# adaLN weights of a diffusion block in wider tiles, with different columns in TensorE's column groups

## The chip, the cores and the metric

One core of a Trainium2 chip runs the whole program. The metric is its device time in microseconds, from the first instruction to the last; lower is better. TensorE does the matrix products, VectorE, ScalarE and GpSimd the work on elements, and SyncE issues the transfers of the weights.

## What is computed

One block of a diffusion backbone, for 256 latent tokens and 256 context tokens of 2048 channels, in float32. The condition c gives six vectors of 2048 by one matrix product (adaLN), a shift, a scale and a gate for the attention and for the MLP:

```
m = silu(c) @ w_ada + b_ada              # w_ada 2048 x 12288; also for c_ctx
shift_a, scale_a, gate_a, shift_m, scale_m, gate_m = split(m, 6)
h = rms_norm(x) * (1 + scale_a) + shift_a        # context: with c_ctx
q, k, v, u = split(h @ w_in)                     # 2048 x 2560
x = x + gate_a * (concat(attention(q, k, v), pooling(u)) @ w_out)
h = rms_norm(x) * (1 + scale_m) + shift_m
x = x + gate_m * (relu(h @ w_up) ** 2 @ w_down)  # hidden 8192
out = rms_norm(x)                                # latent tokens
```

The product with w_ada has only two rows, c and c_ctx, but its matrix is 100 MB, a third of all that is read.

## The kernel before

**Weights** come as one ordered stream of tiles [128, 4, 512] float32, 1 MB each: four row blocks (of 128 rows of the matrix) by 512 columns. Up to five tiles (N_RAW) are in the buffer, and SyncE issues a tile's transfers (L76) when one comes free. A tile of a main product is split in halves ahead of its use: ScalarE makes the high part hi (L89), VectorE or, for every third half of the first 140 tiles, GpSimd the low part lo (L91). A main product is three matmuls, hi by hi, lo by hi, hi by lo (mm3, L280 to L282). An adaLN tile isn't split.

**An adaLN chunk before** is 256 columns of a scale beside the same 256 of a shift, which serves two row blocks of the activations, or 512 columns of a gate. Its four tiles have four row blocks each. On TensorE (ada_pe, L297) a tile is four matmuls of 32 columns of silu(c) by 512 of the weights, one on each column group (tile_position (0, 32 j)), each for another row block; so the four groups hold partial sums of the same 512 columns. After the fourth tile ScalarE copies the bank (ada_e, L303), and four small matmuls by the constant sel (ada_cols, L327, the "column step" below) add up the partial sums and put the columns on the partitions; ada_scale and ada_shift (L332 to L336) finish. For a gate one matmul by the constant selb (L502) adds up and spreads over all partitions instead. On VectorE (ada_dve, L317 and L319) a tile is four operations of 512 columns that add weights times a scalar into ada_v.

**Order of the stages.** The input projection goes through w_in in five groups of row blocks (2, 2, 4, 4, 4), accumulating with VectorE (L428). Among the products of a group stand the adaLN tiles whose scale and shift the next group needs; after a chunk's last one, `modulated` (L445 to L448) scales, shifts and splits two row blocks. Before the last group all 32 attention tiles have been used. The 48 late tiles follow a table, ADA_LATE: MLP chunks 0 and 1 and the gate's four on TensorE, MLP 2, 3, 4, 6 and 7 on VectorE, 5 on TensorE. Of them 4 tiles go beside the last q products, 20 into the attention, 12 into the output projection, 4 behind the first tile of the up projection and 8 further on in it.

The output projection (ps_w) ends in a gate product and an addition for each half of the tokens (t, L816; x, L818), squares (L819), transpositions (L797), the norm's factor spread by a matmul (diag L830, ps_r L832) and copied (rb, L834). `modulate_m` (L846 to L849) makes the MLP's operands mhi and mlo of four row blocks. The first three groups of the up projection run at once, by row blocks, 48 products for each of the twelve tiles, so that the last shifts and scales can come late. The late adaLN tiles of that stage may start only behind rb.

On each engine the order is that of a scheduler, which simulates the program and puts instructions where it expects them to be ready. Each engine then works strictly in that order. TensorE may stand before an instruction that waits, while later ones would be ready.

Of the kernel before, what the change touches and what calls it, by code (L numbers as in the profile page):

```python
# [8 lines left out]
F32 = mybir.dt.float32  # L9
# [42 lines left out]
class WeightStream:  # L52
    """One ordered stream of float32 weight tiles of four blocks [128, 512].

    Tiles are loaded in order, N_RAW deep. Those of the main products are split
    ahead of their use, two blocks at a time, into two float32r parts
    (hi + lo == w exactly).
    """
# [36 lines left out]
    def next(self, kind):  # L95
        """The next tile: the raw one, or W(j, cols) -> the parts of block j."""
# [20 lines left out]
def kernel(  # L117
# [17 lines left out]
    # ------------------------------------------------------------ weight stream  # L135
# [15 lines left out]
    # the input projection's schedule, with the first shift and scale in pairs of row blocks  # L151
    def group_ops(g, pairs):
# [5 lines left out]
        ada = [op for c in pairs for op in [("ada", c, kg) for kg in range(4)] + [("mod", c)]]  # L158
# [8 lines left out]
    in_ops = group_ops(0, [1]) + group_ops(1, [2, 3]) + group_ops(2, [4, 5]) + group_ops(3, [6, 7])  # L167
    last = group_ops(4, [])
    late = [(what, j, kg) for what, j, _ in ADA_LATE for kg in range(4)]

    def add_ada_pair(c_, kg, scale, shift):
# [862 lines left out]
```

## Time and profile before

| | |
|---|---|
| median of 3 runs (1180.76 to 1180.92) | 1180.92 us |
| span of the profiled execution | 1180.8 us |
| TensorE busy | 1128.4 us (96%) |
| VectorE busy | 806.4 us (68%) |
| ScalarE busy | 509.2 us (43%) |
| GpSimd busy | 145.8 us (12%) |
| read and written by transfers | 286.75 MB, mean 243 GB/s |
| chain of work that ended last | TensorE 74%, VectorE 13%, transfers 7% |

In the table the share of busy time is a mean over stages with different limits, so each stage has to be read by itself. The records of matmuls overlap, since they are pipelined; what one costs is the time until the next one's start. A float32 matmul shows as two records. In the rows PE is TensorE, DVE VectorE, ACT ScalarE, POOL GpSimd and PEld the loading of weights into TensorE.

### The profile page before, as it was taken

To read this page: it belongs to the slowest core of one execution; us is meant where nothing else is said; L and a number is where in the kernel's file an instruction comes from. 1 tells how busy PE (TensorE), PEld (TensorE's weight loads), DVE (VectorE), ACT (ScalarE), POOL (GpSimd) and SP (SyncE) were. 2 spreads that over 40 slices of the span, in tenths; PEclk is the share of its full clock that TensorE was granted. 3 is DMA by queue.
4 is the path that set the end of the run, shared out by engine and by line. 5 is a ranking of instruction groups with operands and counts; after the bars stand their busy time and mean duration, and the time that the engine had idled before them with its cause. 6 is when DMAs were issued, how large, how long until landed. Compare 5 with 4: busy or idle time off the path is not lost.

```text
span 1180.8 us, 17728 instructions
## 1 busy us (share of the span) xinstructions
PE 1128.4 (96%) x7140; PEld 952.2 (81%) x7140; DVE 806.4 (68%) x1203; ACT 509.2 (43%) x760; POOL 145.8 (12%) x98
## 2 busy tenths in 40 slices
PE   3999999989999979999999999999999999999996
PEld 2767788746588769988989989989989989988984
DVE  4645468988698888897765765774554554576576
ACT  4633233277633433365434434533533533543452
POOL 1111123610143312320000000000000000000001
PEclk9899999999999979899999999999999999999998
DMA  9999898577898899968675775775566555565532
GB/s 338 312 336 342 279 326 276 178 268 263 272 350 278 288 328 322 319 229 284 243 278 179 249 263 184 254 262 178 179 191 193 187 178 181 185 195 189 179 107 72
DMA packets 174017, 286.75 MB, mean 243 GB/s; under 512 B 5608, under 2 KB 72352, under 8 KB 172784
## 3 DMA queue, kind: packets, MB, share of 16 engines
q1 hardware_dynamic: 172800, 279.55, 70.7%
q0 software_dynamic: 848, 5.55, 1.3%
q8 instruction: 56, 0.92, 0.3%
q10 hardware_dynamic: 288, 0.52, 0.1%
q14 instruction: 25, 0.20, 0.0%
HBM read 283.50 MB, written 2.10 MB: 242 GB/s over the span
## 4 chain that ended last, share of the span: by engine, by line
PE 74%; DVE 13%; DMA 7%; issue 3%; ACT 1%; SPq 1%; POOL 1%; DVEq 0%; ACTq 0%
PE ps_d L282 10%; PE ps_d L281 10%; PE ps_d L280 10%; PE ps_up L282 9%; PE ps_up L280 9%; PE ps_up L281 9%; PE ps_ada L297 4%; DVE ada_v L319 4%; DVE lo L91 4%; DMA raw<-in_w_in_dram 2%; PE ps_qu L280 2%; DMA raw<-in_w_mlp_up_dram 2%; DMA raw<-in_w_out_dram 2%; PE ps_qu L282 2%; PE ps_qu L281 2%
## 5 line engine op out<-in xcount | busy, mean ns | idle before, releaser
L91 DVE TENSOR_TENSOR lo<-raw,hi 128x1024 fp32r<-128x1024 f32 x293 | 376.7, 1300 | 233.5 <-ACT hi L89 233.3
L89 ACT CAST hi<-raw 128x1024 fp32r<-128x1024 f32 x330 | 337.7, 1049 | 416.6 <-PE ps_d L282 159.4
L280 PE MATMUL ps_up<-mhi,hi 128*128 128x256 f32 x1024 | 292.0, 287 | 0.6 <-ACT hi L89 0.6
L282 PE MATMUL ps_up<-mhi,lo 128*128 128x256 f32 x1024 | 289.5, 285 | 1.4 <-DVE lo L91 1.4
L281 PE MATMUL ps_up<-mlo,hi 128*128 128x256 f32 x1024 | 290.1, 284 | 0.0
L281 PE MATMUL ps_d<-lo,ahi 128*128 128x512 f32 x512 | 200.5, 394 | 0.0
L280 PE MATMUL ps_d<-hi,ahi 128*128 128x512 f32 x512 | 200.5, 394 | 0.0
L280 PEld LDWEIGHTS ps_up<-mhi,hi 128*128 128x128 f32 x1024 | 197.4, 193 | 2.7 <-issue 1.8
L282 PE MATMUL ps_d<-hi,alo 128*128 128x512 f32 x512 | 199.5, 395 | 0.0
L282 PEld LDWEIGHTS ps_up<-mhi,lo 128*128 128x128 f32 x1024 | 196.8, 193 | 2.2 <-DVE lo L91 2.1
L281 PEld LDWEIGHTS ps_up<-mlo,hi 128*128 128x128 f32 x1024 | 197.5, 193 | 1.1 <-issue 1.0
L319 DVE SCALAR_TENSOR_TENSOR ada_v<-raw,c_sil,ada_v 128x512 f32<-128x512 f32 x135 | 124.7, 923 | 22.0 <-DMA raw<-in_w_ada_dram 20.1
L91 POOL TENSOR_TENSOR lo<-raw,hi 128x1024 fp32r<-128x1024 f32 x37 | 95.4, 2580 | 336.4 <-ACT hi L89 316.9
L282 PEld LDWEIGHTS ps_d<-hi,alo 128*128 128x128 f32 x512 | 96.5, 188 | 22.4
L280 PEld LDWEIGHTS ps_d<-hi,ahi 128*128 128x128 f32 x512 | 96.5, 188 | 22.2
L281 PEld LDWEIGHTS ps_d<-lo,ahi 128*128 128x128 f32 x512 | 96.5, 188 | 22.1
L280 PE MATMUL ps_qu<-hhi,hi 128*128 128x256 f32 x256 | 75.6, 296 | 5.9 <-ACT hhi L447 5.9
L297 PE MATMUL ps_ada<-raw,c_sil 128*32 128x512 f32 x480 | 74.3, 629 | 2.0 <-DMA raw<-in_w_ada_dram 1.9
L281 PE MATMUL ps_qu<-hlo,hi 128*128 128x256 f32 x256 | 72.7, 285 | 0.0
L282 PE MATMUL ps_qu<-hhi,lo 128*128 128x256 f32 x256 | 72.1, 285 | 0.0
L950 POOL DMA_DIRECT2D fw<-in_final_norm_w_dram x1 | 0.6, 571 | 576.3 <-DVE lo L91 576.3
L280 PEld LDWEIGHTS ps_qu<-hhi,hi 128*128 128x128 f32 x256 | 49.4, 193 | 24.4 <-issue 11.5
(189 smaller groups left out, 1275.2 us busy)
## 6 DMA issues: line engine op xcount, KB each, us to landing
raw<-in_w_ada_dram SPq DMA_DIRECT2D x128, 512.0 KB, 7.7
raw<-in_w_mlp_up_dram SPq DMA_DIRECT2D x64, 1024.0 KB, 5.5
raw<-in_w_mlp_down_dram SPq DMA_DIRECT2D x64, 1024.0 KB, 5.1
raw<-in_w_ada_dram SPq DMA_DIRECT2D x32, 1024.0 KB, 6.6
raw<-in_w_in_dram SPq DMA_DIRECT2D x19, 1024.0 KB, 6.7
raw<-in_w_out_dram SPq DMA_DIRECT2D x16, 1024.0 KB, 7.0
xnat<-in_x_dram SPq DMA_DIRECT2D x2, 1024.0 KB, 6.1
xnat<-in_ctx_dram SPq DMA_DIRECT2D x2, 1024.0 KB, 12.2
```

Of the source, the lines that this page charges most:

```text
L89: nc.scalar.copy(hi, raw)
L91: eng.tensor_tensor(lo, raw, hi.bitcast(F32), ALU.subtract)
L280: nc.tensor.matmul(ps, a[0], b[0], start=first, stop=False, skip_group_check=True)
L281: nc.tensor.matmul(ps, a[0], b[1], start=False, stop=False, skip_group_check=True)
L282: nc.tensor.matmul(ps, a[1], b[0], start=False, stop=last, skip_group_check=True)
L297: nc.tensor.matmul(ps[32 * j : 32 * j + 32, :], c_sil[:, 4 * kg + j, :], raw[:, j, :], start=(kg == 0), stop=(kg == 3), tile_position=(0, ...
L319: nc.vector.scalar_tensor_tensor(box["e"], raw[:, j, :], sc, box["e"], ALU.mult, ALU.add)
L950: nc.gpsimd.dma_start(out=fw, in_=final_w.partition_broadcast(P))
```

## The change

The tiles keep their 1 MB, their number (80) and the places where they stand between the steps. What changes is which part of w_ada a tile holds, and what is done with it.

- **Attention's scale and shift.** Five chunks (ADA_CHUNKS) in place of eight, with the row blocks of the five groups of the input projection: 2, 2, 4, 4, 4. The chunks of two are as before. One of four is 512 columns of the scale beside 512 of the shift, in eight tiles of two row blocks, with rows of 2 KB, not 1 KB. The column groups then hold different columns and, for the two row blocks, two partial sums. `modulated` runs for all four row blocks behind a chunk.
- **Gate.** Sixteen tiles of one row block by all 2048 columns (8 KB rows). Each column group holds 512 other columns and the whole sum. At the end four matmuls of 32 rows, on the four row groups, spread it.
- **MLP's scale and shift.** The first eight row blocks are one chunk "M" of sixteen tiles (1024 columns of each, one row block a tile) on TensorE; the column step is four matmuls for all eight. Blocks 8 to 11 and 12 to 15 are chunks "m" of eight tiles on VectorE, with two operations of 1024 columns a tile in place of four of 512, and a column step of eight matmuls.
- The late table now begins with the gate. So the last 8 tiles of "M" and the first 4 of the chunk for blocks 8 to 11 fall into the output projection, the other 4 of it behind the first up tile. TensorE has 32 of the 48 late tiles (28 before), VectorE 16 (20).
- The buffer t of the gate product has two copies, not three; am and sm keep only the column for c.

```diff
-ADA_LATE = (
-    ("m", 0, "pe"), ("m", 1, "pe"),
-    ("g", 0, "pe"), ("g", 1, "pe"), ("g", 2, "pe"), ("g", 3, "pe"),
-    ("m", 2, "dve"), ("m", 3, "dve"), ("m", 4, "dve"), ("m", 5, "pe"), ("m", 6, "dve"), ("m", 7, "dve"),
-)
+ADA_CHUNKS = ((0, 2), (2, 2), (4, 4), (8, 4), (12, 4))
+ADA_LATE = (("g", 0, 16), ("M", 0, 16), ("m", 8, 8), ("m", 12, 8))
...
-    in_ops = group_ops(0, [1]) + group_ops(1, [2, 3]) + group_ops(2, [4, 5]) + group_ops(3, [6, 7])
+    in_ops = group_ops(0, [1]) + group_ops(1, [2]) + group_ops(2, [3]) + group_ops(3, [4])
...
-    def add_ada_pair(c_, kg, scale, shift):
-        ks = slice(4 * kg, 4 * kg + 4)
-        S.add("ada", *((lambda t, o=o: t[:, :, o : o + 256], w_ada_v[:, ks, col + 256 * c_ : col + 256 * c_ + 256])
-                       for o, col in ((0, scale), (256, shift))))
+    def add_ada_pair(k0, n, i, scale, shift):
+        w, nk = P * n, 8 // n
+        S.add("ada", *((lambda t, o=o: t.rearrange("p a b -> p (a b)").rearrange("p (k c) -> p k c", k=nk)[:, :, o : o + w],
+                        w_ada_v[:, nk * i : nk * i + nk, col + P * k0 : col + P * k0 + w])
+                       for o, col in ((0, scale), (w, shift))))
...
+                S.add("ada", (lambda t: t.rearrange("p a b -> p (a b)"), w_ada_v[:, i, G_A : G_A + D]))
...
             for j in range(4):
                 nc.tensor.matmul(
-                    ps[32 * j : 32 * j + 32, :], c_sil[:, 4 * kg + j, :], raw[:, j, :],
-                    start=(kg == 0), stop=(kg == 3), tile_position=(0, 32 * j),
+                    ps[32 * j : 32 * j + 32, :], c_sil[:, nk * i + j // n, :], raw[:, j, :],
+                    start=(i == 0), stop=(i == steps - 1), tile_position=(0, 32 * j),
...
+    def ada_dve_m(finish):
+            raw = S.next("ada").rearrange("p (k n) c -> p k (n c)", k=2)
+            for j in range(2):
+                sc = c_sil[:, 2 * i + j, 0:1]
...
+                    nc.vector.scalar_tensor_tensor(box["e"], raw[:, j, :], sc, box["e"], ALU.mult, ALU.add)
...
-        for j in range(4):
-            nc.tensor.matmul(ps[:, 2 * j : 2 * j + 2], e[:, 128 * j : 128 * j + 128], weights, start=True, stop=True)
+        n, w = e.shape[1] // P, weights.shape[1]
+        for j in range(n):
+            nc.tensor.matmul(ps[:, w * j : w * j + w], e[:, P * j : P * j + P], weights, start=True, stop=True)
...
-                    nc.tensor.matmul(ps, spread, e, start=True, stop=True)
+        def finish_g(e):
+            for j in range(4):
+                ps = bank("ps_g")
+                r = slice(32 * j, 32 * j + 32)
+                nc.tensor.matmul(ps, selb[r, :], e[r, :], start=True, stop=True, tile_position=(32 * j, 0))
...
+            k0, n = ADA_CHUNKS[op[1]]
+            for p_ in range(k0 // 2, (k0 + n) // 2):
+                modulated(p_)
...
-            t = wop.tile([P, 512], F32, tag="t", name="t", bufs=3)
+            t = wop.tile([P, 512], F32, tag="t", name="t", bufs=2)
```

The order that the scheduler builds, on TensorE where the third group of w_in begins (blocks 4 to 7; ps_k and ps_v are its k and v products). Before:

```order
L280 MATMUL ps_k<-hhi,hi 128x512
L281 MATMUL ps_k<-hlo,hi 128x512
L297 MATMUL ps_ada<-raw,c_sil 32x512 x4
L280 MATMUL ps_k<-hhi,hi 128x512
L281 MATMUL ps_k<-hlo,hi 128x512
L280 MATMUL ps_v<-hi,hhi 128x256 x2
L282 MATMUL ps_k<-hhi,lo 128x512
```

and after:

```order
L281 MATMUL ps_k<-hhi,hi 128x512
L300 MATMUL ps_ada<-raw,c_sil 32x512
L281 MATMUL ps_k<-hhi,hi 128x512
L281 MATMUL ps_v<-hi,hhi 128x256 x2
L300 MATMUL ps_ada<-raw,c_sil 32x512 x3
L282 MATMUL ps_v<-lo,hhi 128x256 x2
L300 MATMUL ps_ada<-raw,c_sil 32x512 x4
L282 MATMUL ps_k<-hlo,hi 128x512
```

The products on the high parts (hhi) now go ahead, two adaLN tiles stand among them, one of them as 1 and 3 matmuls, and the first product on a low part (hlo) comes behind both.

On TensorE in the norm, from the last transpositions to the first up products, before:

```order
L797 MATMUL tp_x<-ident,x_3274 128x128 x8
L832 MATMUL ps_r<-diag,ones 128x256
L327 MATMUL ps_adac<-ones,ada_v 128x2 x4
L297 MATMUL ps_ada<-raw,c_sil 32x512 x16
L280 MATMUL ps_up<-mhi_4045,hi 128x256 x2
L281 MATMUL ps_up<-mlo_4046,hi 128x256
```

and after, with the end of the first up tile:

```order
L836 MATMUL tp_x<-ident,x_3217 128x128 x8
L871 MATMUL ps_r<-diag,ones 128x256
L281 MATMUL ps_up<-mhi_3972,hi 128x256 x2
L282 MATMUL ps_up<-mlo_3973,hi 128x256
...
L283 MATMUL ps_up<-mhi_3987,lo 128x256
L347 MATMUL ps_adac<-ones,ada_v 128x1 x8
L281 MATMUL ps_up<-mhi_3972,hi 128x256
```

The column step and the four tiles ahead of the first up product are gone; the eight matmuls of the column step for blocks 8 to 11 stand behind its 48 products.

On VectorE from the copy of the norm's factor on, before:

```order
L834 COPY rb<-ps_r 128x256
L846 SCALAR_TENSOR_TENSOR x2T_3282<-x2T_3282,am,rb 128x256 x4
L846 SCALAR_TENSOR_TENSOR x2T_3283<-x2T_3283,am,rb 128x256 x4
L332 TENSOR_TENSOR am<-ps_adac,bcol 128x4
L336 TENSOR_TENSOR sm<-ps_adac,bcol 128x4
L849 SCALAR_TENSOR_TENSOR mlo_4046<-x2T_3282,sm,mhi_4045 128x256
L317 TENSOR_SCALAR ada_v<-raw,c_sil 128x512
```

and after:

```order
L873 COPY rb<-ps_r 128x256
L322 SCALAR_TENSOR_TENSOR ada_v<-raw,c_sil,ada_v 128x1024
L885 SCALAR_TENSOR_TENSOR x2T_3225<-x2T_3225,am,rb 128x256 x4
L885 SCALAR_TENSOR_TENSOR x2T_3226<-x2T_3226,am,rb 128x256 x4
L322 SCALAR_TENSOR_TENSOR ada_v<-raw,c_sil,ada_v 128x1024
L888 SCALAR_TENSOR_TENSOR mlo_3973<-x2T_3225,sm,mhi_3972 128x256
...
L322 SCALAR_TENSOR_TENSOR ada_v<-raw,c_sil,ada_v 128x1024 x3
L89 TENSOR_TENSOR lo<-raw,hi 128x1024
L322 SCALAR_TENSOR_TENSOR ada_v<-raw,c_sil,ada_v 128x1024 x3
```

Eight sums of 1024 columns for the column step stand here now, among the operations that make the MLP's operands (x2T, mlo) and one low part of a weight tile.

## Rows read from the trace of the kernel before

**Rows 1.** Windows: start:end and length us; busy PE, PEld, DVE, ACT, POOL (xcount); PEclk, DMA share, GB/s.

```profile
32.00:211.00 179.00, 179.00 (x1304) 137.98 (x1304) 108.18 (x188) 67.25 (x94) 41.28 (x26) 0.99 0.94 312
211.00:250.00 39.00, 31.29 (x213) 23.57 (x212) 38.43 (x83) 17.12 (x44) 19.47 (x23) 0.96 0.55 188
250.00:317.00 67.00, 64.78 (x422) 35.89 (x421) 54.14 (x149) 47.84 (x117) 4.76 (x2) 1.00 0.74 258
317.00:412.50 95.50, 95.41 (x442) 77.66 (x441) 80.86 (x80) 37.91 (x50) 37.34 (x17) 1.00 0.90 310
412.50:430.00 17.50, 10.63 (x50) 5.17 (x50) 14.41 (x44) 5.82 (x14) 0.57 (x1) 0.61 0.94 307
430.00:509.30 79.30, 76.28 (x605) 74.97 (x602) 67.78 (x83) 32.29 (x43) 23.97 (x9) 0.96 0.90 305
```

**Rows 2.** Waits of TensorE, 32 to 211 us: total us, times, longest.

```profile
PE ps_qu L280 <- ACT hhi L447: 5.9, 1, 5.9
```

**Rows 3.** Timeline of TensorE: start us, duration us, instructions; adaLN pieces and a product.

```profile
62.48 1.05 PE L297 MATMUL ps_ada<-raw,c_sil 128*32 128x512 f32 x2
...
76.74 1.06 PE L297 MATMUL ps_ada<-raw,c_sil 128*32 128x512 f32 x8
77.74 0.39 PE L280 MATMUL ps_qu<-hhi,hi 128*128 128x256 f32 x1
```

**Rows 4.** Timeline of TensorE: a column step, a gate matmul, and what follows each.

```profile
177.03 0.95 PE L327 MATMUL ps_adac<-sel,ada_e 128*128 128x2 f32 x8
177.84 0.36 PE L280 MATMUL ps_qu<-hhi,hi 128*128 128x256 f32 x1
...
262.00 1.02 PE L502 MATMUL ps_g<-ada_e,selb 128*128 128x512 f32 x2
262.95 0.64 PE L297 MATMUL ps_ada<-raw,c_sil 128*32 128x512 f32 x4
```

**Rows 5.** Timeline of VectorE: the modulation of two row blocks.

```profile
178.41 1.38 DVE L445 TENSOR_SCALAR xT<-xT,am_a,sm_a 128x256 f32<-128x256 f32 x4
```

**Rows 6.** Timeline of TensorE, 416 to 437 us.

```profile
416.10 2.35 PE L797 MATMUL tp_x<-ident,x 128*128 128x128 f32 x8 [3.69 <-DVE x L818]
...
424.22 6.01 PE L297 MATMUL ps_ada<-raw,c_sil 128*32 128x512 f32 x32
430.16 0.50 PE L280 MATMUL ps_up<-mhi,hi 128*128 128x256 f32 x2
...
436.02 0.95 PE L327 MATMUL ps_adac<-sel,ada_e 128*128 128x2 f32 x8
```

**Rows 7.** Timeline of VectorE, 411 to 431 us.

```profile
411.17 1.22 DVE L91 TENSOR_TENSOR lo<-raw,hi 128x1024 fp32r<-128x1024 f32 x1
412.31 2.32 DVE L319 SCALAR_TENSOR_TENSOR ada_v<-raw,c_sil,ada_v 128x512 f32<-128x512 f32 x3
414.54 0.68 DVE L816 TENSOR_TENSOR t<-ps_w,ga 128x512 f32<-128x512 f32 x1
...
422.83 0.42 DVE L834 COPY rb<-ps_r 128x256 f32<-128x256 f32 x1 [1.31 <-PE ps_r L832]
423.29 3.26 DVE L846 SCALAR_TENSOR_TENSOR x2T<-x2T,am,rb 128x256 f32<-128x256 f32 x8
...
426.60 0.47 DVE L849 SCALAR_TENSOR_TENSOR mlo<-x2T,sm,mhi 128x256 fp32r<-128x256 f32 x1
...
430.24 0.74 DVE L319 SCALAR_TENSOR_TENSOR ada_v<-raw,c_sil,ada_v 128x512 f32<-128x512 f32 x1
```

**Rows 8.** Waits of TensorE, 430 to 509.3 us: total us, times, longest.

```profile
PE ps_up L282 <- DVE lo L91: 1.4, 2, 0.8
PE ps_adac L327 <- DVE ada_v L319: 1.0, 1, 1.0
```

**Rows 9.** Windows, columns as in rows 1: two stretches with different adaLN row lengths.

```profile
60.00:90.00 30.00, 30.00 (x220) 20.29 (x219) 15.06 (x26) 9.57 (x12) 5.16 (x2) 1.00 0.99 336
260.00:265.00 5.00, 5.00 (x29) 2.56 (x28) 3.98 (x9) 4.87 (x9) 0.15 (x1) 1.00 1.05 385
```

More of the change, by code (lines that the diff above doesn't have):

```diff
@@ L157, in group_ops @@
             prod = prod[4:8] + [("ctx",)] + prod[8:] + prod[:4]
-        ada = [op for c in pairs for op in [("ada", c, kg) for kg in range(4)] + [("mod", c)]]
+        ada = [op for c in pairs for op in [("ada", c, i) for i in range(2 * ADA_CHUNKS[c][1])] + [("mod", c)]]
         ops, done = [], 0
@@ L189, in add_in @@
         elif op[0] == "late":
[L190 removed]
+            what, j, i = late.pop(0)
             if what == "g":
[L192 removed]
+                S.add("ada", (lambda t: t.rearrange("p a b -> p (a b)"), w_ada_v[:, i, G_A : G_A + D]))
             else:
[L194 removed]
+                add_ada_pair(j, 8 if what == "M" else 4, i, SC_M, SH_M)
         elif op[0] == "pool":
@@ L254 @@
     sel = const.tile([P, 2], F32, name="sel")
+    sel2 = const.tile([P, 2, 2], F32, name="sel2")
     cols = const.tile([P, P], F32, name="cols")
@@ L282, in mm3, with ada_pe, step @@
         nc.tensor.matmul(ps, a[1], b[0], start=False, stop=last, skip_group_check=True)
-    def ada_pe(finish):
+    def ada_pe(nk, finish):
         box = {}
-        def step(kg):
-            if kg == 0:
+        steps, n = KC // nk, 4 // nk
+        def step(i):
+            if i == 0:
                 box["ps"] = bank("ps_ada")
@@ L371 @@
     nc.vector.tensor_tensor(sel, sel, ident[:, 96:98], ALU.add)
+    for j in range(2):
+        nc.vector.tensor_tensor(sel2[:, j, :], ident[:, 32 * j : 32 * j + 2], ident[:, 64 + 32 * j : 66 + 32 * j], ALU.add)
     nc.vector.tensor_copy(selb, sel[:, 0:1].broadcast_to([P, P]))
@@ L484, in project_qu @@
         accumulate(dst, ps, g == 0)
-    am = const.tile([P, KC, 2], F32, name="am")
-    sm = const.tile([P, KC, 2], F32, name="sm")
+    am = const.tile([P, KC, 1], F32, name="am")
+    sm = const.tile([P, KC, 1], F32, name="sm")
     gate = {}
     def late_steps():
-        for what, j, engine in ADA_LATE:
-            ada, weights, spread = (ada_pe, sel, selb) if engine == "pe" else (ada_dve, ones[:, 0:2], ones)
-            def finish(e, what=what, j=j, weights=weights, spread=spread):
-                if what == "m":
-                    k = slice(2 * j, 2 * j + 2)
-                    ps = ada_cols(e, weights)
-                    ada_scale(am[:, k], ps[:, 0:2], bcol[:, 64 + 2 * j : 66 + 2 * j], cols[:, 48 + 2 * j : 50 + 2 * j])
-                    ada_shift(sm[:, k], ps[:, 2:4], bcol[:, 48 + 2 * j : 50 + 2 * j])
-                else:
-                    ps = bank("ps_g")
-                    nc.tensor.matmul(ps, spread, e, start=True, stop=True)
-                    gs = gate["a"][:, 512 * j : 512 * j + 512]
-                    nc.vector.tensor_tensor(gs, ps, gs, ALU.add)
-            steps = ada(finish)
-            yield from steps[:4]
-            late_finish.append(steps[4])
@@ new lines, in scale_shift @@
+        def scale_shift(k0, scale, shift):
+            n = scale.shape[1]
+            k = slice(k0, k0 + n)
+            ada_scale(am[:, k], scale, bcol[:, 64 + k0 : 64 + k0 + n], cols[:, 48 + k0 : 48 + k0 + n])
+            ada_shift(sm[:, k], shift, bcol[:, 48 + k0 : 48 + k0 + n])
+        def finish_g(e):
[3 more added lines that the diff above has]
+                nc.tensor.matmul(ps, selb[r, :], e[r, :], start=True, stop=True, tile_position=(32 * j, 0))
+                gs = gate["a"][:, 512 * j : 512 * j + 512]
+                nc.vector.tensor_tensor(gs, ps, gs, ALU.add)
@@ new lines, in late_steps, with finish_M, finish_m @@
+        for what, k0, n in ADA_LATE:
+            def finish_M(e, k0=k0):
+                ps = ada_cols(e, ident[:, ::32])
+                for h in range(2):
+                    scale_shift(k0 + 4 * h, ps[:, :, h : h + 1], ps[:, :, 2 + h : 3 + h])
+            def finish_m(e, k0=k0):
+                ps = ada_cols(e, ones[:, 0:1])
+                scale_shift(k0, ps[:, 0:4], ps[:, 4:8])
+            steps = ada_pe(1, finish_g) if what == "g" else ada_pe(1, finish_M) if what == "M" else ada_dve_m(finish_m)
+            yield from steps[:n]
+            late_finish.append(steps[n])
```

41 lines of the change are left out of this document (25 added, 16 removed).

## The prediction

> **What bounds the kernel now.** I read the busy time by stage first, where each row's busy time of TensorE is to be set against the stage's length [rows 1]. TensorE is busy 179.00 of 179.00 us in the input projection, 95.41 of 95.50 in the output projection, 64.78 of 67.00 while the attention goes over into it and 76.28 of 79.30 in the first up projection. There, a matmul more or less is time more or less. Two stretches are otherwise. From 211 to 250 us VectorE has 38.43 of 39.00 us and TensorE 31.29, and in the norm (412.5 to 430 us) TensorE has 10.63 of 17.50 at a mean granted clock of 0.61, since all of it hangs on a chain through VectorE.
>
> Next I asked what TensorE waits for. Between 32 and 211 us there is one wait, at its very start, and none on a transfer [rows 2], though the DMA share is 0.94 there [rows 1]. An adaLN tile that comes sooner is therefore worth nothing by itself; what counts is what the tiles make TensorE and VectorE do.
>
> **Input projection: +5.1 us.** A tile costs TensorE four matmuls, and they take one time together: the piece of one matmul (x2, since the trace shows a float32 matmul as two) lasts 1.05 us and the whole tile (x8) 1.06, with 1.00 from its start to the next product [rows 3]. So the column groups already run side by side, and different columns in place of partial sums change nothing in the price of a whole tile. The rule that I draw: a run of up to four costs about 1.0 us, whatever their number. The number of tiles stays 80. What changes is how the order cuts them. In the built order the input projection has 144 adaLN matmuls before, in runs that need 40 such passes (38 runs, two of them of eight). After, 149 of them (five of a late tile have been pulled ahead) need 49, for in the new groups seven more tiles stand in two pieces between the products, mostly of 1 and 3; two of the 49 belong to the late tile, which the attention saves. 7 passes more by 1.00 are **+7.0**.
>
> Against it, the step that puts columns on the partitions runs for 5 chunks, not 8. One takes 0.95 us, 0.81 until the next product starts [rows 4]: 3 x 0.81 = **-2.4**. The attention's operands are now modulated four row blocks at a time, not two. Four scale-and-shift operations take 1.38 us [rows 5], and I count as much again for the differences behind them, so the fourth block's low part comes some 2.7 us later than in pairs. The order keeps two product groups of the old row blocks (about 6 us, for four blocks; half of that for two) behind the last adaLN tile and lets the first new products go on the high parts, so I take **+0.5** for three such changes of group, with 0 if the cover holds and 1.5 if it fails each time. Sum +5.1, between +4.5 and +6.5.
>
> **Attention: -2.5 us.** In the dense part (250 to 317 us) the order has 64 adaLN matmuls in 20 passes before and 60 in 17 after: -2.5 to -3. One column step goes (-0.8). The gate's four matmuls over 128 partitions with 512 columns, 1.02 us each and 0.95 until the next product [rows 4], of which three stand here, become one run of four over 32 partitions in different row groups. No row shows row groups side by side. At no overlap they cost 4 x 0.95 = 3.8, at the full overlap that the column groups show 1.0; so -2.9 + 1.0 to 3.8. I take 1.5, nearer to the column groups.
> The Trainium skill ("TensorE: Matmul & The Clock Gate", Part 3: Packing small matmuls) gives 3.07x for four matmuls of 32 rows and 512 columns in four row groups; by it they would cost about 3.8/3.07 = 1.2 us, an estimate, and the sum would be 0.3 us lower. No run shown here has such a run of four.
> That makes about -4.6 on TensorE, but VectorE has 54.14 of 67.00 us there and sets the pace from 211 to 250 [rows 1], where the same late tiles fill TensorE's gaps. Gaps filled are worth nothing, so I count half: **-2.5**, between -5 and +2.
>
> **Output projection: +4.2 us.** Before, all its twelve late tiles were VectorE's, and TensorE had two column steps and one gate matmul (2 x 0.81 + 0.95 = 2.6) [rows 4]. After, eight tiles are TensorE's; the order puts six into this dense stage (6 x 1.00) and one column step: 6.0 + 0.8 - 2.6 = **+4.2** (3.7 to 5.2). VectorE loses work here, which TensorE does not wait for.
>
> **The norm: -3.3 us.** TensorE's last product ends 3.69 us before the first transposition, at 412.41 [rows 6]. VectorE then still has a lower part and three adaLN sums (411.17 to 414.54) ahead of the gate's product [rows 7]. With four late tiles on VectorE in that stage, not twelve, that queue is gone and the two gate products and additions follow the last product at once: two of four 0.68 us operations even lie before it. Between -2 and -3.5.
>
> **First up tile: +6.6 us.** Take as zero the start of the copy of the norm's factor (rb), at 422.83 [rows 7]. Before, TensorE fills the time with a column step and four tiles (6.01 us), starts the up projection at 430.16 (+7.3) and ends its first tile and a column step at 436.97 (+14.1) [rows 6]. After, these four tiles are VectorE's: eight operations of 1024 columns. The widths shown are 256 with 0.47 us and 512 with 0.74 [rows 7]; 0.27 for each 256 more gives 1.28. The order puts one of them ahead of the x2T products (3.26 us for eight), one ahead of the low parts (8 x 0.47 = 3.8), then three, one lower part (1.22), three. TensorE's first up tile can start at 0.46 + 1.28 + 3.3 + 1.28 + 0.5 = +6.8, cold; its 48 products take 5.9 us at full clock (430.16 to 436.02) and 9.6 at 0.61, the norm's mean [rows 1]; behind an idle TensorE I take 9.1: end at +15.9. Then comes the new thing: the order has the column step of blocks 8 to 11 at just this place, and it needs all eight sums: 0.42 + 8 x 1.28 + 3.3 + 3.8 + 1.22 = **+19.0**. TensorE waits some 3 us behind it although the next products need nothing of it. It has eight matmuls of one column, twice 0.81: ended at +20.7, against +14.1. The term is **+6.6**; +3 if the sums run ahead of the modulation, +9 if VectorE is late with the lower part.
>
> **The rest of the first up projection: -2.2 us.** The waits in it are 1.4 us for lower parts and 1.0 for the old chunk's sums [rows 8]; VectorE gets through its adaLN work in one piece (16 operations of 1.28 for 32 of 0.74, -3.2 us), so most of both goes. Between -4 and +2. What follows is the same in both orders.
>
> **Sum.** +5.1 - 2.5 + 4.2 - 3.3 + 6.6 - 2.2 = +7.9. The profiled span is 1180.8 us and the median 1180.92, so one stands for the other: 1180.9 + 7.9, **1189 us**.
>
> **The rivals.**
> Transfers bind after all, and wider rows pay: the time ends faster. Where rows of 1 KB prevail (60 to 90 us) the share is 0.99 at 336 GB/s, where the gate's 2 KB rows come 1.05 at 385 [rows 9]; a tile of 1.05 MB would then come in 2.7 and not 3.1 us, and the 24 tiles with 2 KB rows of the input projection would save 9.6 us and hide the passes. Then 1180.9 - 9.6 + 2.8 (the other terms) = 1174. It decides only if TensorE waits for tiles, and rows 2 show that it does not. Chance 0.08.
> The Trainium skill ("DMA: Bandwidth & Descriptors", Why small descriptors are slow) puts a fixed overhead on each packet, which speaks for this change; the two rates agree in sign.
> VectorE's relief is worth more: the eight sums come as fast as the first up tile, without a wait (+0.5 for +6.6), and the later stalls go wholly (-4). Then 1180.9 + 5.1 - 2.5 + 4.2 - 3.3 + 0.5 - 4 = 1181. For it speaks that VectorE has 67.78 of 79.30 us there now; against it the order itself, which puts one lower part and all modulation ahead of the last three sums. Chance 0.14.
> It becomes colder: behind the wait another tile runs at the norm's mean clock of 0.61 (+3.7), the gate's matmuls run one by one (+2.3) and each change of group stalls (+1): about 1196. Chance 0.07.
> Column groups with different columns do not run together. Then 64 tiles would cost three passes more each, over 150 us. The row with eight records in 1.06 us speaks against it. Chance 0.01.
>
> **How the numbers follow.** The forecast (1183.5 to 1195) has 0.70. A measurement can tell about 0.2%, 2.4 us. Faster: the transfers' rival and a little of VectorE's, 0.10. Within 0.2%: the rest of VectorE's and the forecast's lowest edge, 0.14. Slower: 0.76. The range takes in VectorE's rival and the forecast's bounds: 1179.5 to 1195.5.
>
> **What would show it.** In the changed kernel: an input projection some 5 us longer and still without gaps on TensorE; six whole tiles among the products of the output projection; the gate's product right behind the last product; then a wait of about 3 us of the column step on VectorE's adaLN sums behind the first up tile, at half clock at its start. It is wrong if the input projection becomes shorter, or if that column step finds its sums done.

## The result: 1.4% slower, where 0.7% was forecast

The changed kernel takes 1198.32 us (median), the kernel before 1180.92: a ratio of 1.0138 (95% interval 1.0122 to 1.0155), 17.4 us more where 7.9 were forecast, and outside the range that ended at 1195.5. The direction was right, the size was not.

Busy time by stage in the changed kernel, columns as in [rows 1] (start:end and length, then PE, PEld, DVE, ACT, POOL, granted clock, DMA share, GB/s):

```profile
30.50:218.50 188.00, 187.96 (x1291) 138.28 (x1291) 108.26 (x184) 66.45 (x92) 40.17 (x26) 0.99 0.86 306
218.50:250.40 31.90, 26.84 (x180) 18.19 (x179) 31.18 (x61) 10.83 (x30) 20.21 (x23) 1.00 0.58 224
250.40:325.60 75.20, 73.00 (x447) 39.64 (x447) 59.18 (x163) 52.31 (x127) 7.23 (x3) 0.93 0.71 257
325.60:425.90 100.30, 100.30 (x481) 77.14 (x481) 46.51 (x43) 37.83 (x50) 32.54 (x16) 1.00 0.85 301
425.90:434.60 8.70, 1.74 (x10) 0.86 (x8) 6.61 (x23) 2.38 (x6) 0.57 (x1) 0.85 0.33 121
434.60:523.70 89.10, 79.19 (x608) 78.15 (x609) 82.24 (x91) 35.84 (x53) 24.53 (x9) 0.90 0.85 295
523.70:1185.00 661.30, 661.30 (x4042) 588.66 (x4040) 414.62 (x500) 282.19 (x365) 10.85 (x5) 1.00 0.60 201
```

The ends are events that both kernels have: the first ps_qu, ps_s, ps_o, ps_w, the last ps_w, the first ps_up, the first and the last ps_d. Against the kernel before, in us:

| stage | before | after | difference | forecast |
|---|---|---|---|---|
| to the first q product | 31.98 | 30.50 | -1.5 | |
| input projection | 181.59 | 187.99 | +6.4 | +5.1, both |
| first scores to first attention output | 29.32 | 31.89 | +2.6 | |
| to the first ps_w | 74.54 | 75.20 | +0.7 | -2.5, both |
| output projection | 94.98 | 100.27 | +5.3 | +4.2 |
| norm, to the first up product | 17.75 | 8.75 | -9.0 | |
| first up projection | 79.01 | 89.11 | +10.1 | +1.1, both |
| from the first down product on | 671.6 | 673.1 | +1.4 | 0 |

The sum is +16.0 in the spans. The rest lies in the profile of before, which is that of an execution above its median: the runs of that kernel show spans 1.8 us below their times (1178.0 for 1179.78), so a span of 1180.8 belongs to a time of about 1182.6. The -1.5 to the first q product is no gain of the change: three kernels below that keep the old order up to there begin it at 30.6 to 30.8 us.

In the input projection the pieces stand as the order had them, one of x2 for every whole tile that is cut, and cost as much as a whole tile, as in [rows 3] (timeline of TensorE: start, duration):

```profile
107.92 1.06 PE L300 MATMUL ps_ada<-raw,c_sil 128*32 128x512 f32 x8
108.92 0.38 PE L281 MATMUL ps_qu<-hhi,hi 128*128 128x256 f32 x1
...
109.59 1.04 PE L300 MATMUL ps_ada<-raw,c_sil 128*32 128x512 f32 x2
110.57 0.39 PE L283 MATMUL ps_qu<-hhi,lo 128*128 128x256 f32 x1
```

In the norm, VectorE's timeline shows what [rows 7] had in other places: the factor's copy, then the 1024-column sums (1.27 us each) among x2T, mlo and a low part, and below it TensorE's column step, which waits 6.42 us for the last three of them:

```profile
432.00 0.42 DVE L873 COPY rb<-ps_r 128x256 f32<-128x256 f32 x1 [0.79 <-PE ps_r L871]
432.34 1.27 DVE L322 SCALAR_TENSOR_TENSOR ada_v<-raw,c_sil,ada_v 128x1024 f32<-128x1024 f32 x1
433.53 3.25 DVE L885 SCALAR_TENSOR_TENSOR x2T<-x2T,am,rb 128x256 f32<-128x256 f32 x8
436.70 1.28 DVE L322 SCALAR_TENSOR_TENSOR ada_v<-raw,c_sil,ada_v 128x1024 f32<-128x1024 f32 x1
437.89 3.25 DVE L888 SCALAR_TENSOR_TENSOR mlo<-x2T,sm,mhi 128x256 fp32r<-128x256 f32 x8
441.06 3.92 DVE L322 SCALAR_TENSOR_TENSOR ada_v<-raw,c_sil,ada_v 128x1024 f32<-128x1024 f32 x3
445.24 3.04 DVE L89 TENSOR_TENSOR lo<-raw,hi 128x1024 fp32r<-128x1024 f32 x1 [0.27 <-ACT hi L87]
448.21 3.91 DVE L322 SCALAR_TENSOR_TENSOR ada_v<-raw,c_sil,ada_v 128x1024 f32<-128x1024 f32 x3
```

```profile
452.27 3.54 PE L347 MATMUL ps_adac<-ones,ada_v 128*128 128x1 f32 x16 [6.42 <-DVE ada_v L322]
```

### The profile page after: what moved, and what is told of

It reads as the page before. It is cut to its first block, busy times and chain, and to the rows that moved or that the text cites. A ratio compares the mean times of both kernels' runs of the same rounds, so it can differ in the third digit from the quotient of the medians.

```text
span 1196.8 us, 17586 instructions
## 1 busy us (share of the span) xinstructions
PE 1142.6 (95%) x7124; PEld 948.2 (79%) x7124; DVE 771.8 (64%) x1136; ACT 505.6 (42%) x752; POOL 143.4 (12%) x98
## 4 chain that ended last, share of the span: by engine, by line
PE 83%; DVE 7%; DMA 5%; issue 1%; ACT 1%; SPq 1%; POOL 0%; DVEq 0%; ACTq 0%
PE ps_d L282 10%; PE ps_d L283 10%; PE ps_d L281 10%; PE ps_up L282 9%; PE ps_up L283 9%; PE ps_up L281 9%; PE ps_ada L300 5%; PE ps_w L281 3%; PE ps_w L282 2%; PE ps_w L283 2%; PE ps_qu L281 2%; DMA raw<-in_w_mlp_up_dram 2%; PE ps_qu L283 2%; PE ps_qu L282 2%; DVE lo L89 2%
## 5 line engine op out<-in xcount | busy, mean ns | idle before, releaser
L300 PE MATMUL ps_ada<-raw,c_sil 128*32 128x512 f32 x512 | 87.0, 629 | 0.4 <-DMA raw<-in_w_ada_dram 0.4
L338 DVE SCALAR_TENSOR_TENSOR ada_v<-raw,c_sil,ada_v 128x512 f32<-128x512 f32 x60 | 46.3, 771 | 16.1 <-DMA raw<-in_w_ada_dram 15.4
```

The costliest lines, as they stand in the source:

```text
L300: nc.tensor.matmul(ps[32 * j : 32 * j + 32, :], c_sil[:, nk * i + j // n, :], raw[:, j, :], start=(i == 0), stop=(i == steps - 1), tile_po ...
L338: nc.vector.scalar_tensor_tensor(box["e"], raw[:, j, :], sc, box["e"], ALU.mult, ALU.add)
```

## The experiments

Ratios are against runs of the kernel before on the same chip. The theory was the forecast's: the loss is the passes of cut adaLN tiles, the six tiles in the output projection, and VectorE's sums behind the norm. What it did not explain were the attention (+3.3 for -2.5) and the down projection (+1.4).

**The attention's chunks alone.** The late part (ADA_LATE, late_steps, the tiles' loads) is taken from the kernel before.

```diff
-ADA_LATE = (("g", 0, 16), ("M", 0, 16), ("m", 8, 8), ("m", 12, 8))
+ADA_LATE = (
+    ("m", 0, "pe"), ("m", 1, "pe"),
+    ("g", 0, "pe"), ("g", 1, "pe"), ("g", 2, "pe"), ("g", 3, "pe"),
...
```

> Only the attention's scale and shift come in the new chunks (2, 2, 4, 4, 4 row blocks); the late part (gate, MLP) is that of the kernel before. Theory (the cut of the tiles costs TensorE passes): in the built order 47 passes stand in the input projection for 40, and 5 column steps for 8, so +7.0 - 2.4 + about 0.5: 4 to 6 us slower than before, 1185 to 1187 us, and the attention keeps the length that it had before (first ps_s to first ps_w 103.9 us). Rival (the attention became longer because it starts from another end of the input projection, not because of its own late tiles): the attention is longer by some 3 us here too, 1188 to 1190. Second rival (transfers with longer rows pay): no slower than before.

Measured: 1189.58 us, ratio 1.0075 (1.0058 to 1.0092). The first score comes at 217.30 (213.57 before), the attention is 103.8 us long (103.9). By the stages that is the first theory, though the time lies above its range and in that of the rival. The rest of the 8.9 us is mostly the down projection, 2.9 us longer in matmuls that did not change; see the padded kernels.

**The late part alone.**

```diff
-ADA_CHUNKS = ((0, 2), (2, 2), (4, 4), (8, 4), (12, 4))
+ADA_CHUNKS = tuple((2 * i, 2) for i in range(8))
...
-    in_ops = group_ops(0, [1]) + group_ops(1, [2]) + group_ops(2, [3]) + group_ops(3, [4])
+    in_ops = group_ops(0, [1]) + group_ops(1, [2, 3]) + group_ops(2, [4, 5]) + group_ops(3, [6, 7])
```

> Only the late part is new (whole gate rows, wide MLP chunks, engines as in the changed kernel); the attention's chunks are pairs as before. Theory (the parts add up): what the changed kernel lost behind the first attention score stays, so 17.4 less the 4 to 6 of the other half: 11 to 13 us slower than before, 1192 to 1194 us, with the half clock of some 7 us behind the gate's matmuls, the six tiles in the output projection, and the wait of 6 us for the sums of blocks 8 to 11. Rival (the losses need both halves, since the late tiles then start from a later place): 5 to 8 us slower, 1186 to 1189.

Measured: 1191.33 us, ratio 1.0084 (1.0067 to 1.0100), somewhat less than expected. The halves add up: 0.75% and 0.84%, less the address's share that both carry (0.25% and 0.12%, of which the whole change has 0.12%), make 1.34% for 1.38%. In its profile the half clock behind the gate's matmuls lasted 3.4 us and not some 7, and the attention took 103.8 us as before, not 107.1.

**The gate spread over all rows.**

```diff
-                nc.tensor.matmul(ps, selb[r, :], e[r, :], start=True, stop=True, tile_position=(32 * j, 0))
+                nc.tensor.matmul(ps, ident[:, 32 * j : 32 * j + 1].broadcast_to([P, P]), e, start=True, stop=True)
```

> The changed kernel, but the gate is spread by four matmuls over all 128 rows (the weights pick row 32 j) in place of four of 32 rows on the row groups. Theory (matmuls of 32 rows on different row groups ran one after the other, 3.65 us for four, and the clock's fall to half at 288.6 us for 6.8 us, in a stretch without a wait, came from how little of the array they use): the same 3.6 to 3.8 us for the four, no half clock there, and 3 to 3.5 us less than the changed kernel: about 1195. Rival (the clock falls there for another reason, say the adaLN pieces around it): the half clock is there again and the time is the same within 1 us, 1198. If the row groups did overlap at all, this one would be slower by up to 2.5.

Measured: 1196.94 us, ratio 1.0131 (1.0113 to 1.0148), which can't be told from the changed kernel's by time. The traces can: windows of 4 us behind the gate's matmuls, the changed kernel first, then this one:

```profile
288.00:292.00 4.00, 4.00 (x15) 1.02 (x16) 4.00 (x9) 0.81 (x3) 0.00 (x0) 0.58 0.00 0
292.00:296.00 4.00, 4.00 (x22) 1.50 (x19) 1.46 (x8) 0.99 (x4) 0.00 (x0) 0.57 0.79 262
```

```profile
288.00:292.00 4.00, 4.00 (x31) 1.50 (x33) 4.00 (x10) 0.60 (x4) 0.00 (x0) 1.00 0.26 34
292.00:296.00 4.00, 4.00 (x29) 1.62 (x22) 3.07 (x12) 2.87 (x8) 0.00 (x0) 1.00 1.00 367
```

TensorE is busy throughout in both, at about half of its clock in the first and at all of it here, and the stretch from the first attention output to the first ps_w is 72.1 us, not 75.2. But the kernel with the late part alone and the one with the column step held back (below) keep the 32-row matmuls and take 72.2 and 72.0 us there. What these three have in common is 3.4 us at half clock in that stretch, where the changed kernel's profile has 10.2. So the length goes with the time at half clock, and this one trace doesn't show that the 128 rows kept the clock up. The four matmuls cost about the same, 3.54 us for 3.65.

**The weights' buffers back at their old address.** am and sm had become smaller, so every weight buffer lay 96 bytes lower.

```diff
+    gap = const.tile([P, 24], F32, name="gap")
+    nc.gpsimd.memset(gap, 0.0)
```

> The changed kernel with 96 bytes more in the constants (am and sm had become smaller), so that the weights' buffers lie at the addresses that they had before. Theory (the down projection's matmuls of 512 columns, 233.3 ns apart for 232.4 before, 1344 of them, feel the address of the operands): the pace is 232.4 again and the stretch from the first ps_d on 1.3 us shorter, 1196.5 to 1197. Rival (the pace comes from something else, as the place of the other buffers): no change, 1198.

Measured: 1195.78 us, ratio 1.0123 (1.0108 to 1.0138). The stretch of the down and later up projections is 659.96 us long, to the last digit that of the kernel before (509.17 to 1169.13), and 1.4 us shorter than in the changed kernel:

```profile
522.93:1182.89 659.96, 659.96 (x4042) 590.16 (x4040) 414.44 (x501) 282.48 (x365) 10.87 (x5) 1.00 0.61 201
```

**The column step held back**, behind the second tile's last product (mm).

```diff
-LATE_UP = (1,) * 8 + (0,) * 4
+LATE_UP = (0, 2, 1, 1, 1, 1, 1, 1) + (0,) * 4
...
-                with tc.issue_after(rb_ready.ins):
+                with tc.issue_after(rb_ready.ins), tc.issue_after(mm.ins):
                     run_late(LATE_UP[3 * kg + f])
```

> The changed kernel, but the column step of blocks 8 to 11 is queued behind the second tile of the up projection, not the first, and the first two tiles of the next chunk come behind it too. Theory (that wait of 6.4 us is TensorE standing in its queue before a step that nothing near needs, and half of the half clock that follows comes from it): the wait goes, the stretch from the first up product to the first down product is 6 to 8 us shorter, 1190 to 1192 us. Rival (VectorE, busy 82 of 89 us in that stretch, is what bounds it: what isn't waited for here is waited for later, at the low parts or at the last chunk's sums): only 1 to 3 us less, 1195 to 1197.

Measured: 1196.57 us, ratio 1.0133 (1.0114 to 1.0153): the rival. From the last ps_w to the first ps_d it takes 97.7 us, the changed kernel 97.9. TensorE's waits in the first up projection, the changed kernel's and then this one's (us in total, times, longest):

```profile
PE ps_adac L347 <- DVE ada_v L322: 6.4, 1, 6.4
PE ps_up L282 <- DVE mlo L888: 3.3, 2, 3.0
PE ps_up L281 <- ACT mhi L887: 2.8, 2, 2.6
```

```profile
PE ps_up L281 <- ACT mhi L887: 3.8, 1, 3.8
PE ps_up L283 <- DVE lo L89: 3.5, 1, 3.5
PE ps_up L282 <- DVE mlo L888: 2.6, 1, 2.6
```

The wait for the sums is gone, and TensorE waits for the low part behind them instead, and longer for mhi. The place of the step was not the cause of a loss of the size that the theory gives. (TensorE stood at half clock for 23.9 us of these stages, 20.5 in the changed kernel; that can hide some 1.7 us of a gain, by an estimate of half of the difference.)

**Fewer sums on VectorE**, in the chunk of blocks 8 to 11 (some).

```diff
-            for j in range(2):
+            for j in range(1 if some and i >= 4 else 2):
```

> The changed kernel, but of the last four tiles of the chunk for blocks 8 to 11 only the first of the two row blocks is summed on VectorE: four operations of 1024 columns (1.28 us each, 5.1 us) are left out in the norm and behind the first up tile, all else stays. Theory (after the step was held back without a gain: VectorE's sums themselves bound this place, wherever TensorE stands): norm to first down product, 97.9 us, becomes about 5 us shorter, 93 or less, so 1192 to 1194 us. Rival (the place is bound by the chain of the norm and by the low parts of the weights, the sums only happen to be waited for): 0 to 2 us shorter, 1196 to 1198.

Measured: 1191.22 us, ratio 1.0073 (1.0047 to 1.0100). Last ps_w to first ps_d: 91.9 us, 5.9 less for 5.1 us of VectorE's work. Of the 5.9 us, 1.6 are in TensorE's two column steps (3.48 us for 5.10), the first of which ran at half clock in the changed kernel; 4.3 to 5.9 us are then the sums' share. So VectorE's sums themselves bound the time from the norm on. (Windows over these stages, the changed kernel's and this one's.)

```profile
425.90:523.70 97.80, 80.93 (x618) 79.02 (x617) 88.85 (x113) 38.22 (x58) 25.10 (x10) 0.90 0.80 280
```

```profile
424.50:516.40 91.90, 79.98 (x618) 77.91 (x617) 82.75 (x106) 37.51 (x57) 29.91 (x10) 0.91 0.83 286
```

**Passes in the attention left out**, tiles 4 to 9 of the gate, counted from 0 (skip).

```diff
-            for j in range(4):
+            if i in skip:
+                nc.scalar.copy(sink1, raw[:, 0, 0:1])
+            for j in range(0 if i in skip else 4):
```

> The changed kernel, but six of the gate's sixteen tiles (the fifth to the tenth) are loaded and not multiplied: 24 adaLN matmuls fewer, most of them between the first scores and the first attention output, where VectorE is busy 31.2 of 31.9 us (3 passes in place of 8 there in the built order, and 2 fewer ahead of it, 2 fewer behind it). The forecast counted such passes as filling TensorE's gaps, at no price. If that was right: first ps_s to first ps_o stays at 31.5 to 32 us and the run is 3 to 4 us shorter by the four passes elsewhere. If the passes stand in the chain of the attention's stages: 4 to 5 us less there, 27 to 28 us, and 7 to 9 in all, 1189 to 1191.

Measured: 1191.75 us, ratio 1.0081 (1.0052 to 1.0110), but the down projection alone is 6.7 us shorter: the new small buffer (sink1) moved the weights by 32 bytes. Only the stages can be read, first scores to first output and on to the first ps_w, the changed kernel's and this one's:

```profile
218.49:250.38 31.89, 26.84 (x180) 18.18 (x179) 31.17 (x61) 10.81 (x30) 20.21 (x23) 1.00 0.58 224
250.38:325.58 75.20, 73.00 (x447) 39.64 (x447) 59.20 (x163) 52.33 (x127) 7.23 (x3) 0.93 0.71 257
```

```profile
216.97:246.78 29.81, 24.04 (x156) 18.34 (x156) 29.39 (x57) 11.88 (x30) 19.28 (x21) 0.89 0.91 361
246.78:322.42 75.64, 66.91 (x434) 39.03 (x430) 63.31 (x168) 53.53 (x130) 8.35 (x6) 0.98 0.60 218
```

Neither expectation: the first stretch loses 2.1 us, half of the 4.3 us that its passes lost, and the second nothing; there TensorE is now idle for 8.7 us, not 2.2. 7.2 us less adaLN on TensorE (20.1 for 27.3) made the attention 1.6 us shorter. Both stand at half clock for 10.2 us of it, but the changed kernel in the second stretch alone and this one for 6.8 us in the first; so the second stretch can't be compared as it stands.

**Tiles queued whole.** In the input projection each tile's four matmuls are queued behind all products ahead of them in the program, and the later products behind the tile (queue_behind sets an order on TensorE, no wait); the tiles are spread over the first 8 products of a group.

```diff
+                if pin["ada"] is not None:
+                    queue_behind(m.ins, pin["ada"])
+                pin["mm"].append(m.ins)
...
+                if pin["on"] and j == 0:
+                    for x in pin["mm"]:
+                        queue_behind(m.ins, x)
...
-            upto = min(len(ada), -(-len(ada) * (i + 1) // 11))
+            upto = min(len(ada), -(-len(ada) * (i + 1) // 8))
```

On the changed kernel:

> The changed kernel, but in the input projection each adaLN tile's four matmuls are queued together at their place in the program, with no product let past them, and the tiles come somewhat earlier in each group (spread over the first 8 products, not 11). Theory (the new chunks cost there because the order cuts their tiles into pieces): 37 passes for 49 in the stage, of which 2 were those of the late tile; 10 x 1.0 less, and the products are not interrupted inside a group of matmuls (about 1 us): the input projection 9 to 11 us shorter, but the late tile's matmuls (2 us) move behind it: 1189 to 1191 us. Rival (the pieces fill time in which a product would wait for its modulated operand): waits of the products on ACT and VectorE take their place, and the time falls by less than 4, 1194 to 1198.

Measured: 1190.59 us, ratio 1.0102 (1.0067 to 1.0137). The adaLN passes of the stage take 32.9 us, not 45.2, but TensorE is idle for 5.5 us in it where it had not been (the rival's waits, in part); the stage is 7.0 us shorter.

With the old late part and 96 bytes more:

> The attention's scale and shift in the new chunks, with their tiles queued whole as above, the late part that of the kernel before, and 96 bytes more in the constants, so that the weights' buffers lie as before modulo 128 bytes. Theory (wider chunks are good for TensorE where they are not cut: 5 column steps for 8, 37 passes for 40): 2.4 + 3 us less than before in the input projection, the rest as before: 1174 to 1177 us, faster than both kernels. Rival (products wait for the four modulated blocks at each change of group, 1 to 3 us each): 1179 to 1183.

And the kernel before itself, in pairs:

> The kernel before with its chunks in pairs, where only the tiles of the input projection are queued whole and spread over the first 8 products. Theory: 37 passes for 40 but 8 column steps: 3 us less than before, 1177 to 1178; the difference to the kernel with the new chunks is the column steps, 2.4 us. Rival (what is gained comes from the earlier tiles, not from their being whole, or nothing is gained): 1180 to 1182.

Measured: 1168.51 us, ratio 0.9900 (0.9881 to 0.9919), and 1174.64 us, ratio 0.9948 (0.9928 to 0.9967), both faster than expected. But 8.5 us of the first are its down projection, so the pairs were run with 128 bytes more too:

> The kernel before with the input projection's adaLN tiles queued whole and early, and the 128 bytes: neither of the change's parts. If the two effects add: 1174.6 - 8.5 = about 1166 us, faster than the pinned kernel with the wide chunks (1168.5), whose products waited 3.3 us for modulated blocks. If the 128 bytes do nothing by themselves: 1174 to 1175.

Measured: 1166.05 us, ratio 0.9866 (0.9841 to 0.9892), the fastest of all by its median, with neither of the change's parts (its interval just meets that of the wide chunks). TensorE's waits in the input projection, wide chunks (start to 211 us) and pairs (to 206.6 us):

```profile
PE ps_qu L293 <- ACT hhi L499: 5.9, 1, 5.9
PE ps_k L293 <- DVE hlo L500: 3.3, 2, 3.1
```

```profile
PE ps_qu L288 <- ACT hhi L467: 5.9, 1, 5.9
PE ps_k L288 <- DVE hlo L468: 0.6, 1, 0.6
```

Whole tiles help both: with them the wide chunks take 180.2 us for the stage (188.0 in the changed kernel) and the pairs 175.6 (181.6 before). The wide chunks stay behind although they have three column steps less: four blocks that are modulated at once are waited for, and TensorE is idle for 5.7 us in the stage, 1.3 with pairs, and at half clock for 6.9, 4.5 with pairs.

**The address alone**, on the kernel before (128 bytes) and on the changed one (224 bytes), both with hi at 64800:

> The kernel before with 128 bytes more in the constants, so that the weights' buffers lie 128 bytes further (hi at 64800 in place of 64672), nothing else. Theory (the pace of the 512-column matmuls goes by where the operands lie, as in the pinned kernel whose down projection ran at 226.9 ns for 232.4): the stretch from the first ps_d on 8 to 9 us shorter, 1171 to 1173 us. Rival (that pace came with the pinned order or the other chunk sizes): 1180 to 1182.

> The changed kernel with 224 bytes more in the constants, so that hi lies at 64800, where the down projection of the kernel before ran at its best (348.8 us in matmuls for 357.1). Theory (the address is an effect by itself, whatever the order): the down projection 9.8 us shorter than in the changed kernel, 1187 to 1189 us, which is 15 to 17 above the kernel before at that address (1171.6). Rival (part of the change's loss is the address): nearer than 14 to it.

Measured: 1171.59 us, ratio 0.9917 (0.9890 to 0.9944), and 1186.40 us, ratio 1.0028 (1.0016 to 1.0040). The down and later up projections of the padded kernel before:

```profile
508.87:1160.57 651.70, 651.70 (x4042) 589.07 (x4040) 419.06 (x507) 283.45 (x369) 10.04 (x5) 1.00 0.62 206
```

8.3 us less than before without any change in the order. At this address the change costs 1.1% by the two ratios, some 13 us, so the second run comes out as its rival has it: a part of the loss, 1.4 us by the kernel with 96 bytes, is the address.

**Whole gate rows alone**, in the kernel before, spread over 128 rows and over 32:

```diff
-    ("g", 0, "pe"), ("g", 1, "pe"), ("g", 2, "pe"), ("g", 3, "pe"),
+    ("G", 0, "pe"),
...
+                S.add("ada", (lambda t: t.rearrange("p a b -> p (a b)"), w_ada_v[:, kg, G_A : G_A + D]))
```

> The kernel before, where only the gate comes in whole rows of 8 KB (sixteen tiles, the column groups hold different columns), at the same places and on the same engine; it is spread by four matmuls over all 128 rows. The idea of the change alone, with no other order of engines and no chunk of four. Theory (a whole adaLN tile costs TensorE the same whichever columns it holds, and transfers bind nothing): within 2 us of before, 1179 to 1183. Rival (longer rows bring the weights sooner and that is worth something in the attention): 1174 to 1178.

> The same, but the gate is spread as in the changed kernel, by four matmuls of 32 rows on the four row groups. Theory (matmuls of 32 rows let the clock fall): a half clock of 3.4 or 6.8 us begins within 4 us of these four matmuls, as in six of the seven kernels that had them and in none of those without, and the run is 1 to 3 us longer than with 128 rows. Rival (the dips belong to the changed kernel's other late tiles, which stand around them): no dip there, the same time within 1 us.

Measured: 1181.97 us, ratio 0.9996 (0.9980 to 1.0011), and 1181.48 us, ratio 0.9994 (0.9981 to 1.0007). Different columns in the column groups and 8 KB rows, for the gate's sixteen tiles, are worth nothing and cost nothing that could be told (the intervals leave some 2 us). The four gate matmuls here stand in the output projection; over 128 rows they take 3.03 us, over 32:

```profile
328.93 1.14 PE L506 MATMUL ps_g<-ada_e,selb 32*128 32x512 f32 x8
330.00 0.50 PE L280 MATMUL ps_w<-hi,mhi 128*128 128x512 f32 x1
```

1.07 us: all four start within 20 ns. The next fall of the clock is in the norm, at 415 us (two came ahead of them, at 306 and 313 us); so in this trace 32 rows alone do not bring the clock down.

## Why the prediction was wrong, by its own steps

- **Input projection, +5.1: +6.4, at the upper edge of its range (+6.5).** The passes cost +8.8, with two of the late tile (9.0 by the count), the column steps -2.4. The products that were cut into cost 2.4 us more, which the sum lacked. A wait of 2.4 us ahead of the first scores is gone, which it lacked too; but two other kernels with the old input projection wait only 0.3 and 0.5 us there, so that is no sure gain of the change. The cover at the changes of group held.
- **Attention, -2.5: this step failed; +3.3 in the profile.** Three of its terms were wrong. First, the passes ahead of the first output (7.91 us for 4.05) were counted as filler, at nothing; that stretch became 2.6 us longer, and the experiment with fewer passes took back about half of their price. The half that was taken of TensorE's -4.6 had no better ground: 7.2 us less adaLN brought 1.6 there, with VectorE busy for 29.39 of 29.81 us in the first stretch and TensorE idle for 8.73 us in the second.
  Second, the gate's four matmuls took 3.65 us, not 1.5 (285.76 to the next start at 289.41, below). Each writes a bank of its own in PSUM, TensorE's output memory, and in the midst of the attention the loads of their weights waited for what ScalarE had to do first, by the profile's releasers, so they began one after another. The Trainium skill ("TensorE: Matmul & The Clock Gate", Part 3: Packing small matmuls) gives 3.07x; the gate-only pair shows 3.03/1.07 = 2.8x where nothing is waited for, the changed kernel about 1.
  Third, the clock was half for 3.4 us at 251 and for 6.8 us from 288.6 on; the sum had no term for it, and only a rival had the clock colder, in another place. By time at half clock in its second stretch the attention took 103.6 to 103.8 us with 3.4 us (three kernels with this late part; the two that have fewer adaLN passes there are left out; the kernel before, with as much, but in the first stretch, took 103.9), 105.4 with 6.8, 106.1 and 106.3 with about 8.5, and 107.1 with 10.2 in the changed kernel's profile. This holds for this late part only: with the old one and whole gate rows, 9.8 us at half clock went with 104.9. With 3.4 us the change brings the attention as a whole nothing and costs it nothing: the first stretch is 2.2 to 2.5 us longer than before, the second 2.3 to 2.6 shorter. So the dense stretch did save about what was counted, but by luck, since the half had no ground; the passes ahead of it took that back, and the rest of the loss goes with the time at half clock.

The two stretches, up to the first output and to the first ps_w, in the kernel with the column step held back (3.4 us at half clock):

```profile
218.40:250.24 31.84, 26.83 (x179) 18.19 (x179) 31.12 (x61) 10.81 (x30) 20.20 (x23) 1.00 0.57 222
250.24:322.22 71.98, 69.60 (x447) 38.27 (x447) 59.06 (x163) 52.31 (x127) 7.22 (x3) 0.98 0.75 270
```

The gate's tile in the changed kernel: duration min/median/max and first and last start, then what TensorE's matmuls and weight loads (here the loads) waited for ahead of it (us, times):

```profile
L529 PE MATMUL ps_g<-ada_e,selb x8: 587/692/954, 285.8 to 288.5; 32*128 32x512 f32 x8
...
its engine sat idle before it (us, times) until:
  ACT p L738: 0.8, 1
  ACT pT L756: 0.6, 2
  ACT mhi L703: 0.4, 1
```

- **Output projection, +4.2: +5.3.** The six tiles took 5.98 us as forecast; the gate's matmul that went was worth 0.46 and not 0.95. The ps_w products took 0.3 us more (89.0 for 88.7). That this is the address is not shown: with the old late part and the clock full throughout the stage they take 88.7 to 88.8 us at three addresses.
- **Norm and first up projection, -3.3 + 6.6 - 2.2 = +1.1: +1.1**, by errors that cancel. The factor came 4.3 us sooner. The column step ended 23.8 us behind its copy, not 20.7: the low part took 3.04 us and not 1.22, and the step itself 3.54 at half clock. While VectorE made that low part, GpSimd made another (below). Of VectorE's 293 low parts of this size in the trace all 12 that took over 2.4 us overlap with one of GpSimd's; but 11 of the 27 that overlap took less than 1.3 us all the same, so what makes them slow stays open. The rest of the stage then gained 4.3. The cause named, VectorE's sums, was right; that TensorE's place in the queue cost anything was not shown.
- **What follows, 0: +1.4.** The order is the same; the matmuls' pace is not (233.3 ns for 232.4), by the 96 bytes.
- **The base.** A span was taken for the median, 1.8 us too low for the same execution. The forecast adds its sum to the median and isn't moved by it; the sum over the stages is (16.0 for 17.4).
- **The rivals.** Transfers: no sign of it, and the gate-only kernel excludes a gain of more than 2 us from the gate's rows. VectorE's relief: the reverse, its sums bound the stretch behind the norm. The colder clock, at 0.07, came nearest (about 1196): the gate's matmuls did run one by one, and behind the wait the column step stood at half clock. No change of group stalled, and the half clock in the attention it did not have.

In the norm, GpSimd's low part beside VectorE's of 445.24:

```profile
444.40 2.80 POOL L89 TENSOR_TENSOR lo<-raw,hi 128x1024 fp32r<-128x1024 f32 x1 [16.96 <-ACT hi L87]
```

Open is why the clock fell behind the gate's matmuls. Of the eight kernels with these 32-row matmuls in the attention six show a fall that begins within 4 us of their start (the expectation above gave six of seven, where it was five). In these six the four took 3.2 to 3.7 us without a gap. In the other two three of the four overlapped: TensorE was busy with the four for 2.5 us and waited 1.0 and 0.5 us ahead of the last. Where all four ran at once, in 1.07 us, there was no fall, nor with 128 rows. That they run one after another, each on a quarter of the rows, fits all of these; it was not isolated, and each of the cases without a fall rests on one or two traces.

## What to carry to other kernels

Before adaLN-like side work is made coarser, look at what the scheduler does with its pieces: small matmuls that run together cost one pass as a group and one pass each when they are cut apart, and an operand that is ready four blocks at a time is waited for four blocks at a time. Side work on an engine that a serial stretch hangs on (here VectorE in the norm) costs its full time there, wherever its consumer stands; and TensorE time saved in a stretch that hangs on another engine should be counted at a small part. After any change of a buffer's size, compare the pace of matmuls that did not change.

## What the runs showed of the hardware

The pace of the down projection's matmuls, of 512 columns, depends on the byte at which the weights' buffers begin. Its 1536 matmuls took, in us, by the address of the first hi buffer in the partition (that of the activations, ahi, stayed at 182048): 357.1 at 64672, 358.5 at 64576, 360.0 at 64704, 351.8 at 64608, 348.6 to 348.8 at 64800. Not every matmul of that size is sensitive: the output projection's, also of 512 columns, have a median of 227 ns from start to start at all five. Nor are the 256-column ones of the up projection: those behind the first down product took 301.0 or 301.1 us in every kernel. Which distance is good was not worked out; 8.5 us, 0.7% of the kernel, hung on it.
